# Second factors, gate weights and the output's first block on an earlier schedule, in a kernel for an SGU / RWKV-7 / ConvFFN trunk

## The chip, the core and the metric

The kernel runs on one core of one Trainium2 chip. The metric is the device time of one execution in microseconds; three executions were timed, and one more was profiled. The engines are called as in the profile: PE is TensorE (matmul; PEld is its weight load), DVE is VectorE, ACT is ScalarE, POOL is GpSimd, SP is SyncE. ACT and SP also issue the transfers (DMA); in the profile ACTq and SPq mark what stands in these queues. An engine works through its own instructions strictly in the order in which they were put.

## The reference

The trunk has two residual layers on 512 positions of width 1024. Layer 0 mixes with a gated MLP (SGU), layer 1 with RWKV-7, and a gated convolutional FFN follows each. The change lies in the RWKV layer:

```python
def rwkv7_mixer(h, mu, w_r, w_k, w_v, w_o, w0, w1, w2, a0, a1, a2, g1, g2, ...):
    xx = token_shift(h) - h
    xr, xw, xk, xv, xa, xg = (h + xx * mu[i] for i in range(6))
    r, k, v = xr @ w_r, xk @ w_k, xv @ w_v
    w = -softplus(-(w0 + tanh(xw @ w1) @ w2)) - 0.5        # decay, low rank 64
    a = sigmoid(a0 + (xa @ a1) @ a2)                       # low rank 64
    g = sigmoid(xg @ g1) @ g2                              # gate, low rank 160
    kk = normalized heads of k * k_k
    k = k * (1 + (a - 1) * k_a)
    y = wkv7_scan(r, exp(-exp(w)), k, v, -kk, kk * a)      # 16 heads of 64, state 64 x 64
    y = group_norm(y) * ln_w + ln_b + sum(r * k * r_k) * v
    return (y * g) @ w_o
```

## The kernel before

Activations lie transposed: eight tiles `h[k]` of 128 channels by 512 positions. Every fp32 product is made of three matmuls of 128x128 by 128x512 (`mm3`, lines 313 to 315) on a high and a low part of each operand. A high part is a rounding copy on ACT (line 234), a low part a subtraction (line 235), on DVE unless `lo_eng` says otherwise.

Weights come in through two tags of one pool. `w32` has 2 tiles of 128x1024, for weights as they are stored; `w2` has 4 tiles (`WB`) of two halves of 128x512, for a high and low part. The parts of `w_k`, `w_v`, `w_o` and `g1` were made during the FFN before (`make_parts`) and lie in DRAM (`wkd`, `wvd`, `wod`, `g1d`), so that `parts` and `gate_parts` load them ready. A block of keys or values (128 output channels, 24 matmuls of `mm3`) is two `w2` tiles; every third block (`m % 3 == 2`) is two `w32` tiles instead. `Ahead` loads one block ahead of the one that is taken.

`rwkv_first` makes the low-rank inputs (`lowrank`, lines 678 to 689) and the receptance. Its operands come from `mix` (lines 645 to 651): two instructions for the mixed operand, then its high part on ACT and its low part on DVE for even k and on POOL for odd k. `mix` also serves the keys (`r.xk`) and the values (`xv`).

`rwkv_main` then weaves generators. `pairs` goes through eight pairs of heads p: `decay(p)` multiplies the low-rank inputs `r.lr` with the second factors (lines 848 and 850), `operands(p)` forms the scan's operands and stores them to DRAM on SP's queue, `products(p)` makes the triangular blocks (lines 923, 937). The second factors `l2` of two pairs are made at once by `second_factors(p)` for even p, from `decay(p - 1)` on: it takes a `w32` tile, loads on SP's queue (line 755), rounds on ACT (756) and subtracts on DVE (757). `invert` inverts the triangular blocks (lines 999, 1000 on DVE, 1020, 1023 on PE) and `scan` runs eight chunks in each of two groups of heads. Between their steps, `weave` sets matmuls of the generator `fill`: `projections` (eight key blocks, the last two worked together, then eight value blocks), `gates` (the gate's low-rank input, `gate_mix`, its sigmoid, then `gate` for the first group) and `project` (the output, `w_o`, sixteen sums added to `h` in line 1262). `gate_weights(g)` loads half of `g2` into a `w32` tile on ACT's queue (1101, 1102) and makes its parts at once (253 to 255, 234).

A scheduler places the instructions of each engine by their order in the program as priority and by its own estimate of when each is ready; an instruction may be placed ahead of others that stand before it in the program. A tile is handed on when its last reader is done.

Of the kernel before, what the change touches and what calls it, by code (L numbers as in the profile page):

```python
# [20 lines left out]
P = 128  # L21
# [123 lines left out]
class Emit:  # L145
# [137 lines left out]
                        nc.sync.dma_start(dst[:, j, c], x[:, 0:c.stop - c.start].bitcast(F32))  # L283
            yield

    def parts(self, n, m, whole):

        d = self.wd[n][m]
        if whole:
            x = [self.wp.tile([P, 1024], F32, tag="w32", bufs=2, name=self.uid("w32")) for _ in range(2)]  # L290
            for i in range(2):
                self.wq.dma_start(x[i], d[:, i])
            return 1024, [tuple(t.bitcast(F32R) for t in x)]
        return 512, [self.pair(d[:, :, c:c + 512]) for c in (0, 512)]

    def gate_parts(self):

# [324 lines left out]
    def rwkv(self, gain):  # L622
        nc, tc, A = self.nc, self.tc, self.A
        V, S, G = nc.vector, nc.scalar, nc.gpsimd
        with ExitStack() as ctx:
            r = self.r = type("Rwkv", (), {})()
            dp = r.dp = ctx.enter_context(tc.tile_pool(name="rdram", bufs=1, space=DRAM))
            r.hd = [dp.tile([P, T], F32, name=f"hd{p}") for p in range(KT)]


            r.std = [dp.tile([NCH, P, 4, RW], F32, name=f"std{g}") for g in range(2)]
            r.btd = dp.tile([NCH, P, KT, 2, C], F32, name="btd")
            r.vtd = dp.tile([NCH, P, KT, C], F32, name="vtd")
            rp = ctx.enter_context(tc.tile_pool(name="rw", bufs=1))
            r.gc = rp.tile([P, KT, NCH], F32, name="gc")
            r.rt = [rp.tile([P, 4, T], F32, name=f"rt{g}") for g in range(2)]

            r.dq = lambda i, p: self.dpar[:, i, p:p + 1]

            r.ip = ctx.enter_context(tc.tile_pool(name="invert", bufs=1))  # L640
            pctx = ctx.enter_context(ExitStack())
            xp = pctx.enter_context(tc.tile_pool(name="mix", bufs=1))
            r.lr = [xp.tile([P, T], F32R, name=f"lr{i}") for i in range(2)]

            def mix(i, k):

                j = i * KT + k
                t = xp.tile([P, T], F32, tag="mt", bufs=2, name=self.uid("mt"))
                S.activation(t, self.hz[k][:, 0:T], AF.Copy, scale=self.p("mu", j))
                V.scalar_tensor_tensor(t, self.h[k], self.omu[:, j:j + 1], t, ALU.mult, ALU.add)  # L650
                return self.operand(t, lo_eng=(V, G)[k % 2])

            r.mix = mix
            with ExitStack() as actx:
                self.rwkv_first(r, actx.enter_context(tc.tile_pool(name="first", bufs=1)))
            self.rwkv_main(r, pctx, gain)

    def rwkv_first(self, r, ep):

        nc, A = self.nc, self.A  # L660
        V, S, G = nc.vector, nc.scalar, nc.gpsimd
        hx = self.x
# [12 lines left out]
        rb = next(norm)  # L675
        self.dense(lw[1], w, hx[2:], first=False, c0=2 * P)

        def lowrank():
            t, u = tmp("lt", 1), tmp("lu", 1, T + 1)
            G.memset(u[:, 0:1], 0.0)  # L680
            V.tensor_tensor(t, lw[0], rb, ALU.mult)
            V.tensor_tensor(u[:, 1:], lw[1], rb, ALU.mult)
            G.tensor_tensor(t, t, u[:, 0:T], ALU.add)
            S.activation(t[0:64], t[0:64], AF.Tanh)

            for j, x in enumerate(r.lr):
                hi, lo = slice(64 * j, 64 * j + 64), slice(64 - 64 * j, 128 - 64 * j)
                S.copy(x[hi], t[hi])
                V.tensor_tensor(x[lo], t[hi], x[hi].bitcast(F32), ALU.subtract)


        xs = []
        accs = [self.acc() for _ in range(4)]
        for kk in range(4):
            w = self.weights(A["wra"][kk])
# [12 lines left out]
        r.xk = []  # L708
        for m in (0, 2):
            ws = [self.weights(A["wrb"][m + j]) for j in range(2)]  # L710
            accs = [self.acc() for _ in range(2)]
            for k in range(KT):
                for j in range(2):
                    self.mm3(accs[j], self.wcols(ws[j], k * P, P), xs[k], k == 0, k == KT - 1)
                if m == 2:
                    while len(r.xk) < min(k + 3, KT):
                        r.xk.append(r.mix(2, len(r.xk)))
            for j in range(2):
                S.copy(r.rt[1][:, m + j, :], accs[j])

    def rwkv_main(self, r, ctx, gain):
# [26 lines left out]

        def second_factors(p):

            w32 = self.wp.tile([P, 1024], F32, tag="w32", bufs=2, name=self.uid("w32"))
            l2[:] = [ep.tile([P, 2 * P], F32R, tag=f"l2{i}", bufs=1, name=self.uid("l2")) for i in range(3)]
            for j in range(2):
                w = w32[:, 512 * j:512 * j + 2 * P]
                nc.sync.dma_start(w, A["l2"][j][:, P * p:P * p + 2 * P])
                S.copy(l2[j], w)
                V.tensor_tensor(l2[2][H[j]], w[H[j]], l2[j][H[j]].bitcast(F32), ALU.subtract)


        def projections():  # L760

            def loads(n, m):
                return lambda: self.parts(n, m, m % 3 == 2)

            load = Ahead([loads(n, m) for n in PARTS for m in range(KT)])

            def key(m, a):
                while m >= NKEY and m - NKEY not in used:
# [24 lines left out]
            for m in range(KT):  # L793
                a = self.acc("mm")
                w = load.take()
                if m == KT - 1:
                    gw[0] = gate_weights(0)
                for _ in self.dense_steps(a, w, xv):
                    yield
                    next(late, None)  # L800
                    if m == KT - 1 and len(gx) < 2:
                        gx.append(gate_mix(len(gx)))
                for _ in late:
# [80 lines left out]
        def operands(p, u):  # L884
# [17 lines left out]
            V.scalar_tensor_tensor(bk[:, :, 0:C], c3(kn), -0.5, c3(ta), ALU.mult, ALU.mult)  # L902
            V.tensor_tensor(kp, kp, k, ALU.mult)
            V.tensor_tensor(bk[:, :, C:P], c3(kp), c3(ei), ALU.mult)
            G.tensor_tensor(rr, rr, kp, ALU.mult)
            used.add(p)
            S.copy(bk[h1, :, P:], bk[h1, :, 0:C])

# [139 lines left out]
        def gates():  # L1048


            ws = self.gate_parts()
            accs = [self.acc("mm")[0:n] for n in (P, 32)]
            for k in range(KT):
                x = gx[k]
# [10 lines left out]
            for i, a in enumerate(accs):  # L1065
# [6 lines left out]
                else:  # L1072
                    self.stack(r.sg[2], t)
                yield
            while 0 not in normed:
                yield
            for i in range(4):
                gate(0, i, slice(0, T))
                yield
            gated.add(0)  # L1080
            gw[1] = gate_weights(1)

        def gate(g, i, ts):

# [10 lines left out]
            S.copy(oh, o)  # L1095
            V.tensor_tensor(ol, o, oh.bitcast(F32), ALU.subtract)

        def gate_weights(g):
# [3 lines left out]
            self.wq.dma_start(w32[0:32, 512:], A["g2"][P:P + 32, cols])  # L1102
            ws = ep.tile([P, 512], F32R, tag="gw", bufs=1, name=self.uid("gw"))
            self.stack(ws, w32[0:32, 512:], False)
            return (*self.split(ep, w32[:, 0:512], [P, 512], "gw", bufs=1), ws)
# [140 lines left out]

        def project():

            def load(g, m):

                return 512, [self.pair(d[:, :, 512 * g:512 * g + 512]) for d in self.wd["wo"][m:m + 2]]

            ws = Ahead([lambda g=g, m=m: load(g, m) for g in range(2) for m in range(0, KT, 2)] + [self.prefetch])
            for g in range(2):
                while g not in gated:
                    yield
                for m in range(KT):
                    if m % 2 == 0:
                        w = ws.take()
                    a = self.acc("mm")  # L1260
                    yield from self.dense_steps(a, w, outs[g], c0=m % 2 * 512)
                    V.tensor_tensor(self.h[m], self.h[m], a, ALU.add)
                    if g == 1:
                        self.absorb(m, gain)

        def take(gen, n):
            for _ in range(n):
# [9 lines left out]


        fill = itertools.chain(projections(), gates(), project())
        gw = {}  # L1280
# [94 lines left out]
```

## Time and profile before

| | |
|---|---|
| three timed executions | 1302.32, 1304.36, 1302.40 us; median 1302.4 us |
| the profiled execution | 1300.01 us, of it a span of 1298.2 us from the first to the last instruction |
| mean granted PE clock | 0.986 |
| busy, share of the span | PE 98%, PEld 78%, DVE 66%, ACT 49%, POOL 10% |
| DMA over the span | 201.66 MB, mean 155 GB/s |

A row of the timeline gives the start in us from the span's start, the duration in us, the engine, the line of the code, the operation, the output and input by the program's names, the shapes, and in brackets the engine's idle time before it and what ended that. A row of waits gives an engine and the tile and line that waited, what it waited for, the total in us, how often, and the longest. The granted clock is 1.00 at full speed. Matmuls are pipelined, so that the next one starts some 0.23 us after one that is shown as 0.39 us long.

### The profile page before, as it was taken

How to read it: one execution, taken by the hardware profiler on the slowest of the kernel's cores; microseconds unless marked ns; L12 is line 12 of the kernel's file. 1: busy time of each engine (PE TensorE's matmuls, PEld its weight loads, DVE VectorE, ACT ScalarE, POOL GpSimd, SP SyncE). 2: the span in 40 equal slices, each digit the busy share in tenths (PEclk: the TensorE clock that was granted, in tenths of full speed). 3: DMA queues.
4: the chain of work that ended last, by engine and by line, in shares of the span. 5: the costliest groups of instructions: out<-in, count | busy, mean ns of one | idle time of the engine just before them, and what ended most of it. 6: DMA issues, size and time to landing. Idle time of an engine off the chain costs nothing.

```text
span 1298.2 us, 19533 instructions
## 1 busy us (share of the span) xinstructions
PE 1268.4 (98%) x7591; PEld 1018.2 (78%) x7591; DVE 856.2 (66%) x1380; ACT 632.0 (49%) x1084; POOL 129.0 (10%) x140
## 2 busy tenths in 40 slices
PE   9999999999999999899999998999999999999997
PEld 7878888888888888687777766677888888888886
DVE  6465468888885444756779678665677777772233
ACT  6444455556554333565766546532554444442222
POOL 4100100000000000221121022221200000000001
PEclk9999999999999999999999898999999999999998
DMA  7332358877557665235768686964233322333332
GB/s 254 98 109 84 125 172 251 252 247 246 171 168 222 203 208 160 77 121 166 224 183 227 181 227 173 235 179 131 81 107 97 95 95 97 97 93 103 90 90 78
DMA packets 114429, 201.66 MB, mean 155 GB/s; under 512 B 21600, under 2 KB 53600, under 8 KB 114336
## 3 DMA queue, kind: packets, MB, share of 16 engines
q10 hardware_dynamic: 38080, 112.87, 28.7%
q1 hardware_dynamic: 76256, 87.54, 23.0%
q8 instruction: 59, 0.97, 0.3%
q14 instruction: 34, 0.28, 0.1%
HBM read 152.93 MB, written 47.45 MB: 154 GB/s over the span
## 4 chain that ended last, share of the span: by engine, by line
PE 84%; DVE 7%; DMA 1%; issue 1%; ACT 1%; POOL 1%; DVEq 0%; ACTq 0%; POOLq 0%
PE mm L313 9%; PE mm L314 8%; PE mm L315 8%; PE aux L313 6%; PE aux L315 6%; PE aux L314 6%; PE e L314 5%; PE e L315 5%; PE e L313 5%; PE us L313 5%; PE us L315 5%; PE us L314 5%; PE aux L923 1%; DVE tt L1000 1%; PE aux L937 1%
## 5 line engine op out<-in xcount | busy, mean ns | idle before, releaser
L234 ACT CAST w<-w 128x512 fp32r<-128x512 f32 x340 | 206.2, 610 | 372.0 <-PE aux L315 94.8
L235 DVE TENSOR_TENSOR w<-w,w 128x512 fp32r<-128x512 f32 x340 | 232.3, 685 | 195.1 <-ACT w L234 194.7
L313 PE MATMUL mm<-mxh,w 128*128 128x512 f32 (+1 forms) x416 | 173.0, 416 | 2.0 <-ACT mxh L234 1.6
L314 PE MATMUL mm<-mxl,w 128*128 128x512 f32 (+1 forms) x416 | 165.7, 398 | 0.0
L315 PE MATMUL mm<-mxh,w 128*128 128x512 f32 (+1 forms) x416 | 165.5, 398 | 0.0
L340 POOL TENSOR_TENSOR ss<-ss,sq 128x512 f32<-128x512 f32 x30 | 40.2, 1340 | 777.5 <-issue 595.1
L313 PEld LDWEIGHTS mm<-mxh,w 128*128 128x128 f32 (+1 forms) x416 | 78.4, 189 | 22.3 <-issue 3.7
L315 PEld LDWEIGHTS mm<-mxh,w 128*128 128x128 f32 (+1 forms) x416 | 78.3, 188 | 17.7 <-issue 0.8
L314 PEld LDWEIGHTS mm<-mxl,w 128*128 128x128 f32 (+1 forms) x416 | 78.4, 188 | 16.7 <-issue 1.9
L537 ACT ACTIVATE cv<-z,par 128x512 f32<-128x512 f32 x88 | 71.7, 817 | 28.1 <-DVE z L535 22.9
L314 PE MATMUL e<-mxl,w 128*128 128x512 f32 x208 | 81.5, 392 | 3.4 <-POOL mxl L235 1.9
L313 PE MATMUL aux<-mxh,w 128*128 128x512 f32 x216 | 84.6, 392 | 0.0
L313 PE MATMUL us<-mxh,w 128*128 128x512 f32 x216 | 84.6, 392 | 0.0
L315 PE MATMUL aux<-mxh,w 128*128 128x512 f32 x216 | 84.3, 390 | 0.3 <-DVE w L235 0.3
L314 PE MATMUL aux<-mxl,w 128*128 128x512 f32 x216 | 84.2, 390 | 0.0
L314 PE MATMUL us<-mxl,w 128*128 128x512 f32 x216 | 84.2, 390 | 0.0
L315 PE MATMUL us<-mxh,w 128*128 128x512 f32 x216 | 84.1, 390 | 0.0
L313 PE MATMUL e<-mxh,w 128*128 128x512 f32 x208 | 81.7, 393 | 0.3 <-ACT mxh L234 0.3
L315 PE MATMUL e<-mxh,w 128*128 128x512 f32 x208 | 81.1, 390 | 0.0
L538 DVE SCALAR_TENSOR_TENSOR cv<-z,par,cv 128x512 f32<-128x512 f32 x88 | 66.0, 751 | 19.9 <-ACT cv L537 19.9
L539 DVE SCALAR_TENSOR_TENSOR cv<-z,par,cv 128x512 f32<-128x512 f32 x88 | 66.0, 752 | 2.9
L314 PEld LDWEIGHTS e<-mxl,w 128*128 128x128 f32 x208 | 39.1, 188 | 12.9 <-POOL mxl L235 2.7
(1089 smaller groups left out, 2646.1 us busy)
## 6 DMA issues: line engine op xcount, KB each, us to landing
w<-in_wup ACTq DMA_DIRECT2D x88, 512.0 KB, 3.7
w<-in_wdn ACTq DMA_DIRECT2D x32, 512.0 KB, 3.7
st<-std SPq DMA_DIRECT2D x30, 320.0 KB, 5.4
w<-wkd ACTq DMA_DIRECT2D x16, 512.0 KB, 4.9
w<-wvd ACTq DMA_DIRECT2D x16, 512.0 KB, 5.4
w<-wod ACTq DMA_DIRECT2D x16, 512.0 KB, 4.2
w<-in_wdn ACTq DMA_DIRECT2D x16, 384.0 KB, 3.4
w<-in_wsu ACTq DMA_DIRECT2D x8, 512.0 KB, 3.7
```

The costliest lines, as they stand in the source:

```text
L234: nc.scalar.copy(hi[r, :n], src)
L235: (lo_eng or nc.vector).tensor_tensor(lo[r, :n], src, hi[r, :n].bitcast(F32), ALU.subtract)
L313: mm(acc, wh, xh, start=first, stop=False)
L314: mm(acc, wh, xl, start=False, stop=False)
L315: mm(acc, wl, xh, start=False, stop=last)
L340: nc.gpsimd.tensor_tensor(self.ss, self.ss, self.sq, ALU.add)
L537: nc.scalar.activation(c, z[:, 2:], AF.Identity, scale=cw(2, i), bias=self.p("conv_b", l * 44 + i))
L538: nc.vector.scalar_tensor_tensor(c, z[:, 1:T + 1], cw(1, i), c, ALU.mult, ALU.add)
L539: nc.vector.scalar_tensor_tensor(c, z[:, 0:T], cw(0, i), c, ALU.mult, ALU.add)
L923: nc.tensor.matmul(qs[hd][:, c - ch.start, :], bk[H[hd], c, C * hd:C * hd + P], ar[H[hd], c, :], start=True, stop=True)
L937: nc.tensor.matmul(qs[hd][:, c, :], bk[H[hd], c, C * hd:C * hd + P], dg[H[hd], c, :], start=True, stop=True)
L1000: V.tensor_tensor(tt[:, 0:nj, j + 1:32], tt[:, 0:nj, j + 1:32], q, ALU.add)
```

## The change

- `second_factors(p)` no longer loads. `load_l2(p)` takes a `w32` tile and issues the two loads on SP's queue. It is called for pair 0 in `rwkv_first` (behind the last receptance weights), and then by `second_factors(p)` for p + 2.
- `parts` loads every key and value block into two `w2` tiles; no block takes `w32` tiles any more.
- `gate_weights` is divided: `load_gate(g)` loads, `gate_weights(w32)` makes the parts. The first half is loaded one value block earlier, and its parts and the load of `gate_parts` come after the first step of the last value block. The second half is loaded before `gates` begins to wait for the first group's normalized output, and with it the output's first block (`wo.fetch()`), for which `project`'s loader `wo` is made outside of it.
- Three places move from POOL to DVE: the low part of odd operands in `mix` (12 instructions), one sum in `lowrank`, and the product `rr * kp` in `operands` (8 instructions).

```diff
-    def parts(self, n, m, whole):
+    def parts(self, n, m):
         d = self.wd[n][m]
-        if whole:
-            x = [self.wp.tile([P, 1024], F32, tag="w32", bufs=2, name=self.uid("w32")) for _ in range(2)]
-            for i in range(2):
-                self.wq.dma_start(x[i], d[:, i])
-            return 1024, [tuple(t.bitcast(F32R) for t in x)]
         return 512, [self.pair(d[:, :, c:c + 512]) for c in (0, 512)]
+
+    def load_l2(self, p):
+        w = self.wp.tile([P, 1024], F32, tag="w32", bufs=2, name=self.uid("w32"))
+        for j in range(2):
+            self.nc.sync.dma_start(w[:, 512 * j:512 * j + 2 * P], self.A["l2"][j][:, P * p:P * p + 2 * P])
+        self.l2w = [w]
...
-                return self.operand(t, lo_eng=(V, G)[k % 2])
+                return self.operand(t)
...
-            G.tensor_tensor(t, t, u[:, 0:T], ALU.add)
+            V.tensor_tensor(t, t, u[:, 0:T], ALU.add)
...
             ws = [self.weights(A["wrb"][m + j]) for j in range(2)]
+            if m == 2:
+                self.load_l2(0)
...
         def second_factors(p):
-            w32 = self.wp.tile([P, 1024], F32, tag="w32", bufs=2, name=self.uid("w32"))
+            w32 = self.l2w.pop()
...
-                nc.sync.dma_start(w, A["l2"][j][:, P * p:P * p + 2 * P])
                 S.copy(l2[j], w)
                 V.tensor_tensor(l2[2][H[j]], w[H[j]], l2[j][H[j]].bitcast(F32), ALU.subtract)
+            if p + 2 < KT:
+                self.load_l2(p + 2)
...
-            def loads(n, m):
-                return lambda: self.parts(n, m, m % 3 == 2)
-            load = Ahead([loads(n, m) for n in PARTS for m in range(KT)])
+            load = Ahead([lambda n=n, m=m: self.parts(n, m) for n in PARTS for m in range(KT)])
...
-                if m == KT - 1:
-                    gw[0] = gate_weights(0)
-                for _ in self.dense_steps(a, w, xv):
+                if m == KT - 2:
+                    ga["w"] = load_gate(0)
+                for n, _ in enumerate(self.dense_steps(a, w, xv)):
                     yield
                     next(late, None)
+                    if m == KT - 1 and n == 0:
+                        gw[0] = gate_weights(ga["w"])
+                        ga["parts"] = self.gate_parts()
...
-            G.tensor_tensor(rr, rr, kp, ALU.mult)
+            V.tensor_tensor(rr, rr, kp, ALU.mult)
...
-            ws = self.gate_parts()
+            ws = ga["parts"]
...
+            ga["w"] = load_gate(1)
+            wo.fetch()
             while 0 not in normed:
                 yield
             for i in range(4):
                 gate(0, i, slice(0, T))
                 yield
             gated.add(0)
-            gw[1] = gate_weights(1)
+            gw[1] = gate_weights(ga["w"])
```

More of the change, by code (lines that the diff above doesn't have):

```diff
@@ L1096, in gate, with load_gate @@
             V.tensor_tensor(ol, o, oh.bitcast(F32), ALU.subtract)
-        def gate_weights(g):
+        def load_gate(g):
             cols = slice(512 * g, 512 * g + 512)
@@ L1102, in gate_weights @@
             self.wq.dma_start(w32[0:32, 512:], A["g2"][P:P + 32, cols])
+            return w32
+        def gate_weights(w32):
             ws = ep.tile([P, 512], F32R, tag="gw", bufs=1, name=self.uid("gw"))
@@ L1247, in project @@
         def project():
-            def load(g, m):
-                return 512, [self.pair(d[:, :, 512 * g:512 * g + 512]) for d in self.wd["wo"][m:m + 2]]
-            ws = Ahead([lambda g=g, m=m: load(g, m) for g in range(2) for m in range(0, KT, 2)] + [self.prefetch])
             for g in range(2):
@@ L1258, in project @@
                     if m % 2 == 0:
-                        w = ws.take()
+                        w = wo.take()
                     a = self.acc("mm")
@@ L1264, in project, with load_out @@
                         self.absorb(m, gain)
+        def load_out(g, m):
+            return 512, [self.pair(d[:, :, 512 * g:512 * g + 512]) for d in self.wd["wo"][m:m + 2]]
+        wo = Ahead([lambda g=g, m=m: load_out(g, m) for g in range(2) for m in range(0, KT, 2)] + [self.prefetch])
         def take(gen, n):
@@ L1279, in rwkv_main @@
         fill = itertools.chain(projections(), gates(), project())
-        gw = {}
+        gw, ga = {}, {}
         main = pairs()
```

## The prediction

> **What bounds the kernel now.** I read the page first, then the list of who waited for whom on TensorE, then stretches of time with the granted clock, then the timeline at the longest TensorE waits.
>
> ```profile
> span 1298.2 us, 19533 instructions
> PE 1268.4 (98%) x7591; PEld 1018.2 (78%) x7591; DVE 856.2 (66%) x1380; ACT 632.0 (49%) x1084; POOL 129.0 (10%) x140
> PE 84%; DVE 7%; DMA 1%; issue 1%; ACT 1%; POOL 1%; DVEq 0%; ACTq 0%; POOLq 0%
> ```
>
> TensorE (PE) is busy for 98% and carries 84% of the chain that ended last. So a wait is worth something only where PE itself stands still or runs slowly. The change touches the RWKV layer alone, about 519 to 910 us; what PE waits for there is short enough to list (columns: total us, times, longest):
>
> ```profile
> PE aux L1020 <- DVE ix L1005: 4.2, 2, 2.4
> PE e L314 <- POOL mxl L235: 1.9, 2, 1.2
> PE us L1176 <- issue: 1.6, 1, 1.6
> ...
> PE e L848 <- ACT l L756: 1.4, 1, 1.4
> PE e L314 <- DVE mxl L235: 1.3, 1, 1.3
> PE us L1189 <- DMA vu<-vtd: 1.3, 1, 1.3
> ```
>
> Only the second, fourth and fifth rows are work that the change touches: 4.6 us. The clock adds to that. Columns: stretch, its length, busy time (instructions) of PE, PEld, DVE, ACT, POOL, granted PE clock, DMA share, GB/s:
>
> ```profile
> 620.00:640.00 20.00, 20.00 (x169) 15.61 (x167) 15.95 (x25) 13.13 (x26) 3.96 (x4) 1.00 0.93 275
> 642.00:645.00 3.00, 1.57 (x12) 0.91 (x10) 1.97 (x4) 2.01 (x6) 0.00 (x0) 0.97 0.51 136
> 645.00:655.00 10.00, 10.00 (x56) 8.50 (x55) 4.48 (x9) 6.27 (x12) 1.40 (x2) 0.50 0.38 98
> 684.00:726.00 42.00, 41.69 (x309) 32.59 (x308) 40.99 (x95) 25.11 (x55) 3.47 (x5) 1.00 0.88 250
> 730.00:737.00 7.00, 7.00 (x76) 4.67 (x75) 1.44 (x3) 6.13 (x8) 0.00 (x0) 0.51 0.32 76
> 801.00:809.00 8.00, 6.44 (x95) 4.06 (x88) 3.96 (x10) 7.51 (x11) 0.00 (x0) 0.57 0.38 96
> ```
>
> From 645 to 655 us PE runs at half clock with no idle time: 5 us of work lost. From 684 to 726 us VectorE (DVE) is full, 40.99 of 42 us.
>
> **Step 1, the second factors.** Before, `second_factors(4)` asks for a `w32` tile while key block 5 holds both. So SyncE (SP) issues the load only when block 5's matmuls are over, ScalarE (ACT) waits for it, and PE's first decay matmul of pair 4 waits for ACT:
>
> ```profile
> 638.91 3.33 SPq L755 DMA_DIRECT2D w<-in_l  x4
> ...
> 639.36 0.58 ACT L771 COPY key<-mm 128x512 f32<-128x512 f32 x1
> ...
> 643.13 0.40 ACT L756 CAST l<-w 128x256 fp32r<-128x256 f32 x1 [0.94 <-DMA w<-in_l]
> ...
> 643.59 0.49 PE L848 MATMUL e<-lr,l 128*128 128x512 f32 x1 [1.43 <-ACT l L756]
> ```
>
> After the change no key or value block lies in `w32`. `load_l2(4)` is issued when pair 2's factors are taken, so its copies can run right after pair 3's decay matmuls, a whole pair ahead of use. The eight loads on SP are the same eight, only earlier, and SP no longer stands in front of a full tile; what is queued behind them there, the stores of the pairs' operands, can only get earlier. The wait of 1.43 us goes: **-1.4**. What is late next there is only the decay's own chain, which on the pairs before and after is covered by projection matmuls.
>
> The half clock begins about 1.4 us after this wait ends (0.97 up to 645). PE's two longest waits, those for `ix` (2.4 and 1.8), each have a stretch of half clock as well (rows at 730 and 801). Waits of 1.6 and 1.3 us have none (L1176 and L1189). So the length alone does not decide, but no fall stands without a wait. I take the wait as the cause, and the clock to stay up: **-5.0**. Bounds: 0, if it falls anyway; -5.0, all of it.
>
> The Trainium skill ("TensorE: Matmul & The Clock Gate", section "Why this matters for your kernels") speaks against this: it allows idle gaps up to about 3 us before the clock falls, so the 1.43 us should not have done it and the half clock would stay. By that page the sum below would be -4.2 instead of -9.2. The trace sides against that page as far as three falls behind waits of 2.4 us and less can.
>
> **Step 2, GpSimd (POOL) to DVE.** 12 low parts of mixed operands, one add in `lowrank` and 8 products `rr*kp` move: 21 instructions.
>
> ```profile
> 536.50 0.74 DVE L650 SCALAR_TENSOR_TENSOR mt<-h,omu,mt 128x512 f32<-128x512 f32 x1
> ...
> 538.36 0.68 DVE L235 TENSOR_TENSOR mxl<-mt,mxh 128x512 fp32r<-128x512 f32 x1
> 538.96 1.78 DVE L650 SCALAR_TENSOR_TENSOR mt<-h,omu,mt 128x512 f32<-128x512 f32 x1
> ...
> 538.52 1.67 POOL L683 TENSOR_TENSOR lt<-lt,lu 128x512 f32<-128x512 f32 x1 [2.49 <-DVE lu L682]
> 542.21 1.65 POOL L235 TENSOR_TENSOR mxl<-mt,mxh 128x512 fp32r<-128x512 f32 x1 [2.03 <-ACT mxh L234]
> 550.38 1.67 POOL L235 TENSOR_TENSOR mxl<-mt,mxh 128x512 fp32r<-128x512 f32 x1 [5.74 <-ACT mxh L234]
> 552.11 0.50 PE L314 MATMUL e<-mxl,w 128*128 128x512 f32 x1 [0.70 <-POOL mxl L235]
> 695.50 1.78 DVE L904 TENSOR_TENSOR bk<-ss,rb 128x512 f32<-128x512 f32 x1
> L904 DVE TENSOR_TENSOR bk<-ss,rb x8: 678/1771/1789, 596.9 to 710.8; 128x512 f32<-128x512 f32 x8
> L905 POOL TENSOR_TENSOR rt<-rt,ss x8: 1292/1654/1729, 595.2 to 710.6; 128x512 f32<-128x512 f32 x8
> ```
>
> L650 takes DVE 0.74 us alone and 1.78 beside POOL's L683; L904 goes from 0.68 (its shortest) to 1.77 (median) beside L905. So one POOL instruction costs DVE up to 1.1 us, and the moved one will cost 0.68.
>
> In the mixing before 553 us, POOL has three instructions ahead of operand 5's (538, 542 and the first odd operand's); at 1.04 each they stretch DVE by some 3.1. DVE takes on three (3 x 0.68 = 2.0) ahead of operand 5's low part, so it gets there 1.1 us sooner; the low part itself takes 0.68 instead of 1.67: 552.05 becomes 550.0. PE, which waits for it, gains **-2.0**. Bounds: -3.3, all three waits gone (1.9 + 1.3 us in PE's list); +2.7, if DVE takes on four without losing its stretches.
>
> In the full stretch from 684 us two L904 (at 695.5, and the last at 710.8) lose 1.1 each and two products add 0.68 each: **-0.8**; it reaches PE through the wait for `ix`, which closes this stretch. Bounds: -0.8 and +1.4. The rest lies where DVE has idle time (15.95 of 20 us from 620): nothing; with that cover gone, 0.68 each for what POOL does not give back.
>
> **Step 3, key and value blocks in pairs alone.** Two blocks fit, where a third lay in `w32`. A block is then two issues of 0.54 us on ACT instead of two of 0.33: 0.4 us more for each of the four blocks concerned (2 and 5 of keys, 2 and 5 of values), beside PE's work, so nothing; with PE waiting for ACT it would be 1.6. What counts is when the tiles come free:
>
> ```profile
> 612.03 0.33 ACTq L292 DMA_DIRECT2D w<-wkd  x1
> ...
> 629.21 0.54 ACTq L245 DMA_DIRECT2D w<-wkd  x1
> 629.75 0.57 ACT L771 COPY key<-mm 128x512 f32<-128x512 f32 x1
> 634.68 0.39 PE L315 MATMUL mm<-mxh,w 128*128 128x512 f32 x1
> 640.93 0.39 PE L313 MATMUL mm<-mxh,w 128*128 128x512 f32 x1
> w<-wkd ACTq DMA_DIRECT2D x16, 512.0 KB, 4.9
> DMA to landing us min/median/max: 3.7/5.1/9.6
> ```
>
> The tight one is key block 7, worked together with block 6. Before, its first half is issued at 629.21; after, it needs the half of block 5 that PE leaves at 634.7 + 0.4 = 635.1, and lands 4.9 to 5.1 later (medians: the keys' loads, and all loads of that line of code) at 640.0 to 640.2. PE needs it at 640.93: **0**. This counts on the issue being put ahead of its place in the program (after key copy 5, 639.36). Before, that happened: 629.21 is 10 us ahead of that copy. Bounds: 0 and the second rival below. Value blocks follow each other by more than the landing time: nothing.
>
> **Step 4, gate weights and output block.** `load_gate`, `gate_parts` and `wo.fetch` stand earlier in the program, on the same queue of ACT with the same issues; the tiles they need are freed by step 3, so none of them has to wait there in front of the scan's copies.
>
> ```profile
> 760.67 0.62 ACT L253 CAST gw<-w 32x512 fp32r<-32x512 f32 x1 [1.97 <-DMA w<-in_g]
> 772.93 0.53 ACTq L245 DMA_DIRECT2D w<-wod  x1
> L1262 DVE TENSOR_TENSOR h<-h,mm x16: 676/690/691, 857.2 to 919.5; 128x512 f32<-128x512 f32 x16
> w<-wod ACTq DMA_DIRECT2D x16, 512.0 KB, 4.2
> ```
>
> The output's first half block is on its way at 772.93 already, and its first sum comes out at 857.2: earlier is worth **0** (4.2 us if that cover were gone). The gate weights cost ACT 1.97 us of idle time, but no PE wait names them: **0**. Bounds: -2.0, if all ACT's idle time reaches PE through `vt`; 0.
>
> **Sum:** -1.4 - 5.0 - 2.0 - 0.8 = -9.2. The profiled execution took 1300.0 us (1.8 beyond its span), so 1290.8 for it. It ran 2.4 below the median of the three runs, 1302.4; so I forecast 1302.4 - 9.2 = **1293.2**.
>
> **Rivals.**
> The half clock stays, or falls as long elsewhere: -4.2, 1298.2. For it: waits of 1.3 and 1.6 us without a fall. Against: all three falls stand behind a wait.
> Key block 7 takes the place of the wait removed (the slower side). If ACT issues its load at its place in the program, after the copy at 639.36 + 0.58 = 639.9, it lands at 645.0 to 649.5 (landing 5.1 to 9.6), so PE stands 4.1 to 8.6 us from 640.93, and the clock falls as it does now: 9.1 to 13.6 instead of 6.4. It outweighs step 2 (2.8) from a landing of 5.2 us on; at 7.4 the time is 1302.4 + (6.4 + 5.0 - 6.4) - 2.8 = 1304.6. For it: half the depth, and DMA engines busy at 0.93 ahead of it. Against: the early issue shown above.
> DVE becomes the bound of the mixing, with four instructions more and its stretches kept: +2.7 instead of -2.0, 1297.9. For it: that POOL is what stretches them is inferred from overlap alone. Against: L904's median of 1771 ns against 678 for its shortest.
> The change does not do what it says: the factors' copies keep their place in ACT's queue, and step 1 gives nothing: -2.8, 1299.6. Against: nothing but the tile held them.
>
> **How the numbers follow.** Forecast 0.45 (own range 1290 to 1296), clock 0.2, block 7 0.18, DVE 0.1, no effect 0.07. Less than 0.2% (2.6 us; the runs shown spread over 2.0) can't be told from nothing. Faster by more: 0.45, the clock case, most of DVE and half of no effect, less something for what I do not see: 0.72. Slower by more needs block 7 at a late landing: 0.12. Same: 0.16. The range runs from 1288 (all mixing waits gone, 1.3 more, the gates' 2.0, and some 2 of the 3.4 us that the half clock takes at 730) to 1304, which leaves out the later landings of block 7.
>
> **What would show it.** Right: no PE wait for `l` at L848; clock 1.00 behind it; L904 and the mixing's L650 at 0.7 us throughout; PE's waits for `mxl` under 1.5 us in sum; gate and output rows earlier with PE's list otherwise unchanged. Wrong: a PE wait for a load `w<-wkd` at the start of the joint key blocks; a new stretch at half clock; DVE waits for `mxl` above 3 us.

## The result, and the profile after

The changed kernel took 1292.34 us (median of 4 runs, 1290.99 to 1294.26) against 1302.36 (1301.33 to 1304.36) for the kernel before: ratio 0.9927, 95% interval 0.9913 to 0.9941. Run again later, beside the experiments below, it took 1293.33 against 1300.16 (0.9953, 0.9938 to 0.9969). The forecast was 1293.2.

The page of the changed kernel: span, busy time, and the shares of the chain that ended last.

```profile
span 1292.4 us, 19533 instructions
PE 1269.4 (98%) x7591; PEld 1018.9 (79%) x7591; DVE 852.8 (66%) x1401; ACT 631.3 (49%) x1084; POOL 97.7 (8%) x119
PE 88%; DVE 5%; ACT 1%; POOL 0%; issue 0%; DMA 0%; DVEq 0%; ACTq 0%; POOLq 0%
```

PE now carries 88% of the chain instead of 84%, DVE 5% instead of 7%. POOL has 21 instructions less, DVE 21 more, and yet DVE is busy 3.4 us less (852.8 for 856.2): what it took over is more than paid by the instructions that POOL no longer stretches. This execution took 1294.26 us, the longest of the first four runs; the profiled one of before took 1300.01, less than any of those four. So the two profiles differ by 5.8 us where the medians differ by 10.0. Where the rest lies is told under "Two parts of a time".

Line numbers behind the new function are shifted by 2 to 10. What PE waits for (total us, times, longest):

```profile
PE e L315 <- ACT mxh L234: 2.4, 1, 2.4
PE aux L1025 <- DVE ix L1010: 1.6, 2, 1.1
PE mm L315 <- ACT mxh L234: 1.6, 1, 1.6
...
PE mm L316 <- DVE mxl L235: 0.2, 1, 0.2
```

The wait for `l` is gone. Those for `mxl` fell from 3.2 to 0.2, those for `ix` from 4.2 to 1.6. The first row is new: 2.4 us at one place, in the mixing. Two rows that the prediction took to be untouched, `issue` (1.6) and `vtd` (1.3), are gone as well. In other profiles such rows come and go (in a second profile of the changed kernel `vtd` has 0.8 again), and no experiment says why. Stretches of time, with the same columns as in the prediction:

```profile
645.00:655.00 10.00, 10.00 (x81) 7.63 (x78) 9.62 (x16) 9.57 (x18) 0.11 (x1) 1.00 0.59 156
684.00:726.00 42.00, 41.33 (x336) 31.81 (x332) 39.06 (x86) 23.06 (x50) 0.61 (x2) 0.96 0.82 232
690.00:697.00 7.00, 6.86 (x49) 5.91 (x46) 6.96 (x18) 4.01 (x9) 0.00 (x0) 0.76 0.60 184
734.60:738.00 3.40, 3.40 (x74) 3.15 (x66) 0.62 (x1) 1.09 (x3) 0.00 (x0) 1.00 0.38 90
738.00:748.20 10.20, 10.20 (x86) 8.05 (x86) 2.11 (x1) 6.12 (x11) 2.36 (x4) 0.50 0.65 157
799.40:806.30 6.90, 6.76 (x112) 5.10 (x104) 1.69 (x4) 4.60 (x8) 1.23 (x2) 0.51 1.05 202
```

From 645 to 655 the clock stays at 1.00. But there is half clock at 693.6 (3.4 us), at 738 (10.2) and at 799 (6.8): 20.4 us between 600 and 900, where before had 23.8 (10.2, 6.8, 6.8). A second profile of the same changed kernel (run 9 below) has 17.1: 6.8 at 735 and 10.2 at 793, and none between 600 and 735. And in the 3.4 us before 738 PE is busy without a break. The timeline at the places that the prediction names:

```profile
566.42 7.05 SPq L295 DMA_DIRECT2D w<-in_l  x6
...
623.62 0.71 ACT L759 CAST l<-w 128x256 fp32r<-128x256 f32 x2 [0.34 <-PE e L853]
635.53 0.53 ACTq L245 DMA_DIRECT2D w<-wkd  x1
636.52 0.73 PE L853 MATMUL e<-lr,l 128*128 128x512 f32 x2
...
753.60 0.60 ACT L253 CAST gw<-w 32x512 fp32r<-32x512 f32 x1
...
765.91 0.54 ACTq L245 DMA_DIRECT2D w<-wod  x1
```

Six of the eight loads, those of pairs 0, 2 and 4, go out from 566.42 on, so pair 4's goes out earlier still than the prediction said (when pair 2's factors are taken, copied from 596.91 on). Pair 4's factors are copied at 623.62, right after pair 3's matmuls, and its own decay matmuls run at 636.52 instead of 643.59, with no wait in brackets. Block 7's first half is issued at 635.53; the joint key blocks have no wait for it. The gate weights' first load goes out at 650.49 instead of 755.13, their copy waits for nothing, and the output's first half block is issued 7.0 us sooner.

**Two parts of a time.** A run's span times its granted clock is what it would take if the clock never fell (while PE is the bound): its work at full clock. The rest, span times one less the clock, is lost to the clock. The kernel before (51 runs, from three series): work 1280.1, lost 20.0. The changed kernel (10 runs): work 1277.0, lost 14.7. So it gained 3.1 (standard error 0.5) in the one and 5.3 (0.7) in the other, 8.4 together. The split is rough: over the runs of each kernel, 79% of the spread of the span goes with the second part, but at 0.68 us of span for each us lost (least squares, all series pooled), probably because some of the half clock lies where PE would have waited anyway (argued, not shown). By that slope the 5.3 are worth 3.6, and 4.8 fall to the first part; where PE is busy throughout, they count in full.

### The profile page after: what moved, and what is told of

It reads as the page before. It is cut to its first block, busy times and chain, and to the rows that moved or that the text cites. A ratio compares the mean times of both kernels' runs of the same rounds, so it can differ in the third digit from the quotient of the medians.

```text
span 1292.4 us, 19533 instructions
## 1 busy us (share of the span) xinstructions
PE 1269.4 (98%) x7591; PEld 1018.9 (79%) x7591; DVE 852.8 (66%) x1401; ACT 631.3 (49%) x1084; POOL 97.7 (8%) x119
## 4 chain that ended last, share of the span: by engine, by line
PE 88%; DVE 5%; ACT 1%; POOL 0%; issue 0%; DMA 0%; DVEq 0%; ACTq 0%; POOLq 0%
PE mm L315 10%; PE mm L316 9%; PE mm L317 9%; PE aux L315 6%; PE aux L317 6%; PE aux L316 6%; PE e L316 6%; PE e L315 6%; PE e L317 5%; PE us L317 5%; PE us L315 5%; PE us L316 5%; PE aux L928 1%; PE aux L942 1%; PE us L1186 1%; PE us L1199 1%
## 5 line engine op out<-in xcount | busy, mean ns | idle before, releaser
L317 PEld LDWEIGHTS mm<-mxh,w 128*128 128x128 f32 (+1 forms) x416 | 78.7, 189 | 18.1 <-issue 1.2
L539 ACT ACTIVATE cv<-z,par 128x512 f32<-128x512 f32 x88 | 71.7, 817 | 28.8 <-DVE z L537 23.8
L315 PEld LDWEIGHTS e<-mxh,w 128*128 128x128 f32 x208 | 39.1, 188 | 11.3 <-ACT mxh L234 3.3
```

The lines of the kernel that those rows point to most:

```text
L315: mm(acc, wh, xh, start=first, stop=False)
L317: mm(acc, wl, xh, start=False, stop=last)
L539: nc.scalar.activation(c, z[:, 2:], AF.Identity, scale=cw(2, i), bias=self.p("conv_b", l * 44 + i))
```

## The experiments

The table gives what each measured; the last two columns are differences against the kernel before in the same series (means, us). The standard errors of a difference (the scatter to expect of it) are 0.4 to 1.0 in work and 0.7 to 1.6 in clock.

| kernel | median | ratio, 95% | work | lost to clock |
|---|---|---|---|---|
| 1 POOL to DVE alone | 1299.06 | 0.9982 (0.9966-0.9998) | -3.4 | +1.0 |
| 2 loads and tiles alone | 1294.56 | 0.9948 (0.9935-0.9962) | -2.3 | -4.8 |
| 3 key block 5 alone | 1297.30 | 0.9966 (0.9953-0.9979) | -0.7 | -4.6 |
| 4 gate loads put back | 1292.73 | 0.9935 (0.9919-0.9950) | -3.8 | -5.0 |
| 5 low-rank later | 1291.92 | 0.9919 (0.9896-0.9941) | -6.1 | -4.5 |
| 6 POOL to DVE, key block 5 | 1295.73 | 0.9969 (0.9949-0.9989) | -3.9 | -0.6 |
| 7 wait filled | 1296.53 | 0.9959 (0.9944-0.9974) | +0.2 | -5.4 |
| 8 small matmuls filled | 1292.91 | 0.9935 (0.9916-0.9954) | +3.3 | -12.3 |
| 9 changed kernel again | 1293.33 | 0.9953 (0.9938-0.9969) | -3.5 | -2.9 |
| 10 factors loaded at use | 1293.20 | 0.9942 (0.9930-0.9954) | -4.8 | -2.7 |
| 11 low-rank later, filled | 1290.39 | 0.9923 (0.9910-0.9935) | -5.6 | -4.4 |
| 12 the same, filled twice | 1293.53 | 0.9945 (0.9926-0.9964) | -5.7 | -1.4 |

**1. The moves from POOL to DVE alone.**

```diff
-                return self.operand(t, lo_eng=(V, G)[k % 2])
+                return self.operand(t)
-            G.tensor_tensor(t, t, u[:, 0:T], ALU.add)
+            V.tensor_tensor(t, t, u[:, 0:T], ALU.add)
-            G.tensor_tensor(rr, rr, kp, ALU.mult)
+            V.tensor_tensor(rr, rr, kp, ALU.mult)
```

> The kernel before with only the 21 instructions moved from GpSimd (POOL) to VectorE (DVE): low parts of the odd mixed operands, one add in the low-rank step, the products rr*kp. Weights and loads stay as before. Theory (the prediction's step 2): 2.8 us below before, 1299.6, and the waits for mxl of 3.2 us in sum fall under 1.5; the half clock behind the wait for l (10.2 us long, at about 645) stays. From the two profiles alone the mixing gained only 0.95 us up to the receptance, so a second theory: 1 to 1.5 below before, with a new wait of some 2.4 us for mxh near 545 in place of the waits for mxl. Rival: DVE becomes the bound, 2 or more above before.

Waits of PE, and then two stretches of time:

```profile
PE e L313 <- ACT mxh L234: 2.4, 1, 2.4
PE aux L1020 <- DVE ix L1005: 2.3, 2, 1.3
...
PE e L848 <- ACT l L756: 1.5, 1, 1.5
```

```profile
640.00:643.40 3.40, 1.93 (x14) 1.09 (x12) 2.33 (x5) 1.99 (x6) 0.00 (x0) 1.00 0.48 145
643.40:653.70 10.30, 10.30 (x54) 8.49 (x55) 5.24 (x10) 6.12 (x12) 0.11 (x1) 0.50 0.36 91
```

3.4 us less work, and nothing gained in clock (2.4 us less in the mean time): the wait for `l` stays, and the half clock behind it. In the mixing the waits for `mxl` are replaced by one of 2.4 for `mxh`, as in the changed kernel; the wait for `ix` fell by 1.9. DVE did not become the bound.

**2. The loads and tiles alone** (the changed kernel with the three lines of 1 put back).

> The changed kernel with the three moves from POOL to DVE undone: only tiles, loads and blocks of key and value weights differ from before. Theory (the prediction's step 1): 6.4 us below before, 1296.0; no wait of PE for l, no half clock near 645. Rival (the half clock falls elsewhere instead): 1.4 below before or less, with as many us of half clock in the whole span as before. If it and the POOL part add up, their gains against before sum to 10.0.

4.8 us less lost to the clock and 2.3 less work, 7.1 in the mean: the theory, with a little more. Its profile has no half clock near 645, and 17.1 us of it between 600 and 900 (at 668, 730 and 798) instead of 23.8. In mean time, 1 and 2 add up to about the whole change (2.4 and 7.1, for 8.4). But their work (3.4 and 2.3) does not add up to the whole change's 3.1: both shorten the same wait for `ix` (2.3 us left in 1, 2.7 here, 1.6 with both), and the new wait for `mxh` comes with the first alone.

**3. Key block 5 alone in pairs.**

```diff
-                return lambda: self.parts(n, m, m % 3 == 2)
+                return lambda: self.parts(n, m, m % 3 == 2 and (n, m) != ("wk", 5))
```

> The kernel before with one edit: key block 5 alone is loaded as two half blocks of the pair tiles, so that the w32 tiles are free when the second factors of pair 4 are asked for. Theory: this wait is the whole worth of the loads' part, so 6.4 us below before, the same as the kernel with all of the loads' part; PE does not wait for l and the clock stays up at 645. Rival 1: the gain comes from the other blocks or from the early issue of the second factors too, then it gains clearly less (1 to 3) than that kernel. Rival 2: key block 7, now loaded later with block 6 from the pair tiles, makes PE wait, and the time is as before or above.

```profile
636.61 0.73 PE L848 MATMUL e<-lr,l 128*128 128x512 f32 x2
```

```profile
645.00:655.00 10.00, 10.00 (x82) 7.72 (x80) 9.69 (x13) 6.73 (x13) 3.54 (x2) 1.00 0.68 181
```

This one block frees the tile. The decay matmuls run at 636.61 without a wait, the clock stays up, and 4.6 us less are lost to it. It is nearly all of the clock's gain, got without any load moved in the program. The time of 2 isn't reached: 1297.30 for 1294.56, 1.8 more in the mean (standard error 0.9), nearly all of it in work (-0.7 for -2.3). So the rival that the other blocks and loads have a share is not excluded. Key block 7 made nobody wait (rival 2 falls).

**4. The gate and output loads put back to their old places** (`load_gate`, `gate_parts` and `wo.fetch` where they were before).

> The changed kernel with the gate weights' loads and the fetch of the output's first block put back at their old places in the program. Theory (the prediction's step 4 at nothing): the same as the changed kernel within 1 us, 10.0 below before. Rival: the earlier loads are worth up to 2.0 us, so it is 8.0 below before, and ACT's idle time ahead of the gate weights' split (1.97 us) is back and reaches PE through vt.

The gate weights' first load in time, in the changed kernel, in the kernel before, and in this experiment:

```profile
650.49 0.34 ACTq L1108 DMA_DIRECT2D w<-in_g  x1
```

```profile
755.13 0.36 ACTq L1101 DMA_DIRECT2D w<-in_g  x1
```

```profile
652.42 0.34 ACTq L1103 DMA_DIRECT2D w<-in_g  x1
```

Its ratio is 0.9935 where the changed kernel's are 0.9927 and 0.9953. But the loads did not go back in time: with the tiles free, the scheduler issued the first one at 652.42, ACT's wait of 1.97 did not return, and the output's first half block went out at 767.82 (changed 765.91, before 772.93). So only the place in the program is shown to be worth nothing; what late gate loads would cost is not tested by this run.

**5. The low-rank step later.**

```diff
-            if kk == 1:
+            if kk == 3:
                 lowrank()
```

> The changed kernel with the low-rank step's call put behind the fourth pair of mixed operands instead of the second. In the changed kernel DVE does that step's work (1.4 us in one piece) ahead of mixed operand 4, and PE waits 2.4 us for mxh near 545, where before it waited 3.2 us for mxl. Theory: the wait of 2.4 goes and nothing takes its place, so 1 to 2.4 below the changed kernel, 11 to 12.4 below before. Rival: DVE is simply full up to 553, the same work is late at the next operand, and the time is that of the changed kernel, 10.0 below before, within 1.

The timeline at the new wait and up to the first copy of the receptance, in the changed kernel, in the kernel before, and in this experiment:

```profile
543.00 1.39 DVE L691 TENSOR_TENSOR lr<-lt,lr 64x512 fp32r<-64x512 f32 x2 [0.50 <-ACT lr L690]
544.42 1.42 DVE L701 SCALAR_TENSOR_TENSOR h<-h,par,rb 128x512 f32<-128x512 f32 x2
545.21 1.38 ACT L651 ACTIVATE mt<-h,par 128x512 f32<-128x512 f32 x2 [1.72 <-DVE h L701]
547.81 0.50 PE L315 MATMUL e<-mxh,w 128*128 128x512 f32 x1 [2.40 <-ACT mxh L234]
557.40 0.59 ACT L708 COPY rt<-e 128x512 f32<-128x512 f32 x1 [1.18 <-PE e L317]
```

```profile
541.26 0.74 DVE L699 SCALAR_TENSOR_TENSOR h<-h,par,rb 128x512 f32<-128x512 f32 x1
542.03 2.38 DVE L689 TENSOR_TENSOR lr<-lt,lr 64x512 fp32r<-64x512 f32 x2
545.71 0.75 DVE L699 SCALAR_TENSOR_TENSOR h<-h,par,rb 128x512 f32<-128x512 f32 x1
...
558.35 0.59 ACT L706 COPY rt<-e 128x512 f32<-128x512 f32 x1 [1.57 <-PE e L315]
```

```profile
544.41 1.41 DVE L701 SCALAR_TENSOR_TENSOR h<-h,par,rb 128x512 f32<-128x512 f32 x2
...
554.30 0.57 ACT L708 COPY rt<-e 128x512 f32<-128x512 f32 x1
```

In the changed kernel DVE idles 0.5 us for the low-rank copy, spends 1.39 on its low parts, and only then scales the next two `h`; before, one of these had been scaled ahead of it (541.26). ACT waits 1.72 for them, and PE 2.40 for ACT. So of 3.0 us of waits removed 2.4 came back, and the receptance is through 0.95 sooner than before (557.40 for 558.35). With the step later this wait is gone, nothing in the mixing takes its place, and the copy comes at 554.30, 3.1 sooner still. Later on, the waits for `ix` are 3.0 in its profile instead of 1.6; in 11 and 12, with the same step, they are 2.0 and 1.4. Work falls 2.6 below the changed kernel's (9), about what the theory had. The ratio, 0.9919, is not told apart from the changed kernel's first 0.9927, and its interval just overlaps that of the second; the means (1291.6, and 1293.6 over the changed kernel's ten runs) differ by 2.0, with a standard error of 1.3.

**6. POOL to DVE and key block 5** (edits 1 and 3 together).

> The kernel before with the 21 instructions moved from POOL to DVE and key block 5 alone loaded in pairs; the other blocks, the second factors' loads and the gate loads as before. Theory: these two small edits are all that the change is worth, so the time of the changed kernel, 9 to 10 below before. Additivity of the single edits measured so far (3.2 and 5.0) gives 8.2 below. Rival: the remaining moves (other blocks in pairs, loads ahead of use) carry 2 or more of the gain, so it is 8 or less below before.

Its work is that of the changed kernel (-3.9), so these two edits hold all of that part. But the clock's gain is not: three of its twelve runs lose 27 to 29 us and the other nine 14.2 to 20.7, and its mean is 4.5 below before where the median is 6.5. In the profiled one (1304.58) PE stays at half clock for 30.7 us in a row; its first, second and last stretches of 3.4 us:

```profile
719.00:722.40 3.40, 2.22 (x42) 1.70 (x41) 3.38 (x2) 0.00 (x0) 0.00 (x0) 1.00 0.93 245
722.40:725.85 3.45, 3.45 (x40) 2.41 (x38) 1.52 (x3) 3.02 (x3) 0.00 (x0) 0.50 0.20 53
...
749.70:753.10 3.40, 3.40 (x38) 2.33 (x37) 0.00 (x0) 1.45 (x4) 0.00 (x0) 0.50 0.55 153
```

It begins with a wait of 1.2 us for `ix`, and then goes on with PE busy throughout. So what the rest of the change seems to add is a steadier clock: its ten runs lose 12.9 to 18.1. What does it is open. The other three blocks in pairs are one candidate, the transfers that start earlier because of them the other: here the first gate load goes out at 757.91 and ACT waits 2.15 for it, and 4 and 10 issue their loads when the changed kernel does, so they exclude nothing. And 3, which is this kernel without the moves from POOL, has none of the long losses in its seven runs (10.3 to 18.2).

**7. The wait filled.** In the kernel before, ahead of pair 4's decay matmuls:

```diff
+            for _ in range(6 if p == 4 else 0):
+                nc.tensor.matmul(accs[0], r.lr[0][:, 0:P], r.lr[0], start=True, stop=True)
```

> The kernel before with six extra 128x512 matmuls, whose result is overwritten, ahead of pair 4's decay matmuls: they fill the wait of 1.43 us for l with work of the full array, and nothing else changes. In all profiles so far the clock changes only at whole multiples of 3.41 us, and it falls behind a window in which the full array had little to stream. Theory (an empty window brings the fall): the half clock at 645 goes, 4 to 5 below before, though PE does not start its decay matmuls sooner. Rival 1 (the order of the work there brings it, or the fall only moves to a later place): as before within 1. Rival 2: the extra matmuls do not fall into the wait and cost their 1.4 us: 1.4 above before.

```profile
637.78 1.65 PE L848 MATMUL e<-lr 128*128 128x512 f32 x6
...
644.94 0.50 PE L850 MATMUL e<-lr,l 128*128 128x512 f32 x1 [0.56 <-ACT l L756]
```

```profile
645.00:655.00 10.00, 9.98 (x91) 7.63 (x92) 7.87 (x15) 8.58 (x17) 1.40 (x2) 1.00 0.47 123
```

The six ran 7 us ahead of the wait and pushed dense work into it: 0.56 us of it are left. The work did not change (+0.2), the clock stays at 1.00, and 5.4 us less are lost to it. The decay matmuls start no sooner (644.94 for 643.59), so it is the little work in that time that lowered the clock, and not what starts late behind it.

**8. Small matmuls filled.** In the changed kernel, ahead of four groups of 32x32 matmuls of the inverse:

```diff
+                    for _ in range(2 if i != g else 0):
+                        nc.tensor.matmul(ps, self.c("ident", P), self.c("smask", T), start=True, stop=True)
```

> The changed kernel with two extra 128x512 matmuls (constants, result overwritten) ahead of each of four groups of 32x32 matmuls of the triangular inverse: eight in all, at about 0.46 us each 3.7 us of PE time, about half of it in waits that PE has there. At 737 us the changed kernel's profile has 10.2 us of half clock that no wait precedes, only some 5 us of 64x64 and 32x32 matmuls with PE busy throughout; at 799 another 6.8. Theory (a window of 3.41 us in which the array is mostly unused lowers the clock, busy or not): both stretches go or get short, 8 us of half clock or more are saved, 4 us of time, so 1 to 3 below the changed kernel. Rival (only idle time of PE lowers the clock, the stretch at 737 has another cause): half clock as in the changed kernel, and the time 2 to 3.7 above it.

What PE does in the changed kernel right before its clock falls at 738, then, of the experiment, a row of the timeline and a stretch of time:

```profile
734.21 0.69 PE L1028 MATMUL aux<-li,tt 32*32 32x32 f32 x32
734.83 1.66 PE L942 MATMUL aux<-dg,bk 64*128 64x64 f32 x13
...
736.76 0.69 PE L1028 MATMUL aux<-li,tt 32*32 32x32 f32 x32
```

```profile
734.01 1.98 PE L1020 MATMUL aux<-cst 128*128 128x512 f32 x4
```

```profile
738.00:748.00 10.00, 10.00 (x133) 7.14 (x133) 2.93 (x3) 7.03 (x15) 2.36 (x4) 1.00 0.43 104
```

The half clock at 738 is gone, and only 8.2 us are lost to the clock in the mean, against 14.7 in the changed kernel. But here two extra matmuls take 1.98 us, each recorded as two, and not 0.9: eight cost some 7.5, and the work rose by 6.3 above the changed kernel's. The sum is no gain. The theory of the clock held; the price was put at half.

**9. The changed kernel again**, as the measure for the next three.

> The changed kernel itself, run again as the measure for the three below: 1292 to 1293, 9 to 10 below before, and 14 to 16 us of its span lost to the lowered clock (span times one less the granted clock, as a mean over its runs) against 20.5 in before.

**10. The second factors loaded at use** (in `second_factors`, with all blocks in pairs).

> The changed kernel with the second factors' loads issued where they are used, as before, and not a pair ahead; all blocks stay in pairs, so the w32 tiles are free. Theory (only the tile held the load back; the issue is put early anyway once the tile is free): the same as the changed kernel within 1, 10 below before, no PE wait for l. Rival (the loads ahead of use carry their own share of the 2 to 3 us that blocks and loads are worth beyond key block 5): 1.5 or more above the changed kernel, with waits of ACT or PE for the factors.

The first six loads in its profile:

```profile
567.19 7.05 SPq L295 DMA_DIRECT2D w<-in_l  x6
```

The same as the changed kernel (1293.20 and 1293.33), and PE has no wait for `l`. But the loads ran no later either: six go out from 567.19 on (changed kernel 566.42), because the scheduler issues them early once a tile is free. So the place of the loads in the program is worth nothing, and a free tile is all it took; a load that really comes at use was not tested.

**11 and 12. Low-rank later, with cheaper extra matmuls** at the first inverse (two of 0.23 us ahead of two groups), and in 12 one more of constants ahead of two groups of the second.

> The changed kernel with the low-rank step behind the fourth pair of operands, and with two extra 128x512 matmuls at 0.23 us each (result overwritten) ahead of each of two groups of 32x32 matmuls of the first inverse, where the clock fell in every profile of the changed layout (near 735). By the measured parts: 2.9 us less work at full clock from the first, 0.9 more from the extra matmuls, and 3 to 4 us less lost to the clock: 4 to 6 below the changed kernel, 1286 to 1288. Rival (the fall moves to a later window, or the array is filled too little): only the first part's 2, 1290 to 1291.

```profile
729.70:733.10 3.40, 3.40 (x55) 2.93 (x54) 0.68 (x1) 1.45 (x2) 0.00 (x0) 1.00 0.50 132
733.10:746.80 13.70, 13.70 (x132) 10.61 (x131) 3.41 (x6) 6.22 (x12) 2.38 (x4) 0.50 0.61 140
```

> As the one before it, and one more extra matmul of constants (0.46 us) ahead of each of two groups of 32x32 matmuls of the second inverse, near 795, where PE has waits of its own. Theory: 1 more of work, 2 to 3.4 less lost to the clock, so 1 to 2.4 below the one before it. Rival: the windows there are too empty for one extra matmul each (0.1 to 0.2 of the array's rows in use), and it costs its 0.9.

In the profile of 11 the clock fell all the same, as its rival had it: the cheap ones seem to fill too little (last section). What is gained is the low-rank step's: 2.1 us of work, and 1290.39 against 1293.33, the best of the series (its interval, 0.9910 to 0.9935, lies below the changed kernel's 0.9938 to 0.9969 of the same series, but not below that of its first runs; the mean is 2.9 below that of the ten runs, standard error 0.9). 12 keeps the work and gains nothing in clock; 1293.53 is not told apart from the changed kernel.

## Why the prediction was right, point by point

**The wait for `l` (-1.4)** went as forecast, and nothing was late next.

**The half clock at 645 (-5.0).** The size was right where it stands alone: 7 fills that wait and changes little else, loses 5.4 us less to the clock and is 5.2 shorter in the mean. In the whole change 5.3 less is lost, worth 3.6 to 5.3. The wait was the cause of this fall: in 7 PE starts no sooner, and only the time that was empty is filled. But the reason given, "no fall stands without a wait", is false. At 738 the clock fell with PE busy throughout, and 8 held it up by giving the array more to do. So the gain is one of averages: the profiled pair shows 23.8 and 20.4 us of half clock, worth 1.7, and whoever had only these two would have called the step a miss. The first rival (the fall moves elsewhere) is what that one pair looks like, and a sign of being wrong that was named, a new stretch at half clock, is there at 693.6; the runs refute the rival all the same, with 14.7 us lost in the mean for 20.0.

**The mixing (-2.0)** was mis-sized: 0.95. That the waits for `mxl` would go (3.2 to 0.2) was right, and POOL's stretching too. The step that failed is "552.05 becomes 550.0. PE gains": it followed operand 5's low part alone. In the changed kernel DVE puts the low-rank step's 1.39 us ahead of the next two `h`, where before one of these had been scaled already; operand 4's high part became the late one. 5 shows this, by taking that step away.

**The full stretch (-0.8)** was mis-sized the other way. The wait for `ix` at its end was 2.42 before; it is 0.96 in 1 and 0.52 in the whole change. But it is also 1.65, 1.60 and 1.49 in 2, 3 and 7, which move nothing from POOL, so some 0.8 of the whole change's fall need not be POOL's. (The prediction said first that the change touches no row of `ix`, and then let this step reach PE through it.) In sum step 2 came to -3.4 in work for -2.8, and to -2.4 in the mean time of 1. That POOL's end is what gives DVE its time back is shown by the groups of the changed kernel (busy us, mean ns):

```profile
L652 DVE SCALAR_TENSOR_TENSOR mt<-h,omu,mt 128x512 f32<-128x512 f32 x24 | 17.7, 748 | 0.4 <-ACT mt L651 0.2
L909 DVE TENSOR_TENSOR bk<-ss,rb 128x512 f32<-128x512 f32 x8 | 5.5, 684 | 0.0
L910 DVE TENSOR_TENSOR rt<-rt,ss 128x512 f32<-128x512 f32 x8 | 5.5, 683 | 0.0
```

The second had a median of 1771 ns before. The Trainium skill ("SBUF — State Buffer", section "Who interferes with whom") says that a DVE instruction with two inputs in SBUF contends with a GpSimd instruction that reads SBUF; the trace agrees, 684 ns in the mean for a median of 1771.

**Pairs alone (0).** Block 7's load was issued at 635.53 (forecast 635.1), and no PE wait names it. The second rival did not come.

**Gate and output loads (0).** Not contradicted: no PE wait names the gate weights, neither with the early loads nor before, in 3 or in 6, where ACT waits 2.0 to 2.3 for them. It isn't tested by itself, since in 4 the loads ran early all the same.

**The sum.** Waits and DVE: forecast -4.2, measured -3.1 to -4.8. Clock: -5.0, measured -5.3 to -3.6. The first four runs showed -10.0 in the median, all ten -8.4 in the mean; -9.2 lies between. That the sum came out so close is in part luck: inside step 2 two errors of about 1 us cancel, two waits of 2.9 in sum went that were not counted, and the clock term had the right place and size on a reason that does not hold in general.

**Open:** what in the rest of the change steadies the clock (6 against the changed kernel), what late gate loads cost, and where between the two bounds given below the clock's decision lies.

## What to carry to other kernels

Split every run's time by its granted clock before comparing two profiles: here most of the scatter of one kernel, and about half of the gain, was clock, and one pair of profiles told it wrongly. A short wait of the matmul engine can cost several times its length through the clock; look for it where little else is queued, and remove it by freeing the tile that holds the load back (one block did it; the load's place in the program made no difference, because it was issued at the same time either way). Before an experiment that moves a load is read, look in its trace whether the load moved in time. When work moves to a shared in-order engine, follow all that is queued there, the neighbour's operand too, and not only the instruction that was late.

## What the runs showed of the hardware that was not expected

**The clock is decided on a fixed grid.** In all 14 profiles it falls and rises only at whole multiples of 3.413 us. In the kernel before, the first fall is at 20.18 and the others at 644.81, 730.15, 801.83 and 1289.93: 183.0, 208.0, 229.0 and 372.0 times 3.413 later. The Trainium skill ("TensorE: Matmul & The Clock Gate", section "Part 1: The HAM clock gate (the "warmup" mystery)") states a window of 3413 ns that runs freely and does not start with the kernel; the traces agree that the grid does not start with the kernel: the first fall, in work that no edit touches, is at 20.18 in before and at 21.19 in the changed kernel. That runs of one kernel lose 12.9 to 18.1 us fits it, since the same gap may fill one window or be split over two; no run shows this by itself.

**What counts is how much of the array a window uses, not whether PE is busy.** For every window of the 14 traces I summed the columns of its matmuls, each times the share of the 128 rows that it uses (a matmul on the edge of a window counts by the part of its time that lies inside; the fall at each kernel's end is left out). A window at full clock has 7,529 of these (median). Of those below 1,800, 27 of 27 were followed by half clock; between 1,800 and 2,600, 24 of 58; above, 3 of 5,049. PE's busy time sorts them worse: 12 of these 54 falls came behind a window in which it was busy throughout. The window before the fall at 644.8 had 1,713 (the wait), the one before 738 had 1,419 (64x64 and 32x32 matmuls without a break), the one before the fall in 11 had 1,858. In 7 the two windows from 643.6 to 650.4 have 4,233 and 2,598, and the clock stays. The same page's section "Why this matters for your kernels" allows gaps up to about 3 us; here 1.43 us of idle time in thin work was enough, and none at all at 738.

**Half clock holds itself.** At half clock, 50 of 52 windows below 2,600 were followed by another, and none of 39 above 3,000. Mixed work that passes at full speed falls below the bound when it runs at half: nine windows in a row in 6.
